# A one-core graph attention kernel: tables built during the first sort, the first load ahead of the other bins, counts read early, bf16 weight pairs and 121-wide sums

## The chip, the cores and the metric

The kernel runs on one core of a Trainium2 chip. The metric is device time in microseconds (us) of one execution.

An execution's time and its profiled span are two numbers. The span runs from the first to the last record that the profiler took; the time includes a little more. Stages are compared by spans, kernels by times.

## The reference

Four attention heads over 4,096 nodes with 64 features, and 50,000 random edges.

```python
for h in range(4):
    x_proj[h] = x @ weight[h]
src_att = sum(x_proj[h, src] * att_src[h]);  dst_att = sum(x_proj[h, dst] * att_dst[h])
score   = src_att + dst_att;  score = where(score > 0, score, 0.2 * score)
for each edge:  output[h, dst] += exp(score) * x_proj[h, src]
output[h, dst] /= (sum of exp(score) over the edges into dst) + 1e-8
```

## The kernel before

The edges become fp32 keys, 128 runs of 512, and are sorted on VectorE in two stages, with a gather of windows from memory between them, so that in the end each of 34 blocks of 121 destinations finds its edges in sixteen windows of 128, one for each group of 256 sources. Each block loads its edges, makes one-hot matrices on VectorE, gathers the source rows on TensorE with them, weighs the rows on VectorE, and sums them by destination on TensorE.

What each name in the profile is: `cnt` bounds of the windows; `raw`, `kr` the input of the second sort; `bc` a block's edges, copied to all partitions; `oh` its one-hots; `xps` gathered rows; `wv` the weights exp(score); `val` weighted rows; `Sb` the turned one-hot; `acc` the sums; `pf` the sums times the weight matrix; `res` the output rows.

```python
with tc.manual_schedule():                      # the constants above stand outside: a scheduler places them
    ...
    so.rows(1, EL)                              # first sort
    store(skey1, so.runs())
    tables(pr, pps, pp1)                        # x, weights -> xa, adb: 32 transposes, 132 small matmuls
    bounds(so1, pp1, sgn, ...)                  # cnt_ps on TensorE, cnt, ws, we on VectorE
    ...
    for i in range(NI - 1):                     # four bins of eight blocks
        win.unpack(i)                           # VectorE, then two stores on SyncE
    blocks.run(lambda: win.unpack(NI - 1))      # loads 0 to 2 first, the fifth bin after turn(0)
n1 = nc.values_load(most[0:1, 0:1], ...)        # overflow counts, read at the very end
n2 = nc.values_load(most[0:1, 1:2], ...)
with tc.If((n1 > W1) | (n2 > W2)): ...          # not taken with these edges
# --- one block, run() ---
for b in range(ND):
    self.load(b + 3); self.weigh(b); self.gather(b + 1); self.turn(b + 1); self.onehot(b + 2)
    if b: self.sink.give(b - 1)
    self.scatter(b)
# --- cuts from its parts ---
V.tensor_tensor(out=wv[:], in0=av(ex[:], 0, [1, H], [2 * H, NT], [0, 2]), ..., op=OP.max)     # fp32 ex
T.matmul(out=acc[:, k * P:(k + 1) * P], lhsT=val[:, t, k * P:(k + 1) * P], rhs=Sb[:, t, :], ...)  # 128 wide
V.tensor_scalar(out=inv[:], in0=aT[:, C:CW], scalar1=1e-8, ...); V.reciprocal(out=inv[:], in_=inv[:])
```

## Time and profile before

| | before |
|---|---|
| time, median of the first three runs | 372.82 us |
| time of the profiled run, its span | 373.68, 371.9 us |
| first sort stored | at 72.49 us |
| second sort can begin (`kr`) | at 124.91 us |
| first bin stored, first one-hot | at 169.96, 180.71 us |
| one block of the loop on VectorE | 5.26 us |

Read it in stages. Up to 72.5 us VectorE sorts, and beside it little works but ScalarE and GpSimd in the first 20 us. From there to 125 us VectorE does next to nothing. From 181 us on, a loop of 34 blocks keeps VectorE and TensorE both nearly full. A share of busy time over the whole span (VectorE 76%, TensorE 58%) shows none of this. The lines themselves stand in the prediction.

### The profile page before, as it was taken

Reading aid. Unit: us, or ns where it says so; the run is one execution under the profiler, and the core shown is the slowest. Engines: PE = TensorE matmul, PEld = TensorE weight load, DVE = VectorE, ACT = ScalarE, POOL = GpSimd, SP = SyncE. Lnnn points to the kernel's source line nnn. Section 1 sums busy time; section 2 is a strip of 40 time slices with the busy share of each in tenths; the row PEclk is TensorE's granted clock in tenths of the full one; section 3 lists DMA queues with packets and bytes.
Section 4 is the critical chain, followed back from the end, with each engine's and each line's share of the span. In section 5 each row is a group of like instructions: output and inputs, shape, how many; then the busy total and the mean of one; then the engine's idle time right before and its main releaser. Section 6 shows DMA issues by size and latency. Waiting matters only on the chain.

```text
span 371.9 us, 9662 instructions
## 1 busy us (share of the span) xinstructions
PE 215.6 (58%) x4122; PEld 206.5 (56%) x4122; DVE 282.4 (76%) x584; ACT 164.3 (44%) x290; POOL 18.9 (5%) x40
## 2 busy tenths in 40 slices
PE   0000000029996000000399999999999999999990
PEld 0000000016996000000399999999999999999980
DVE  4999999700002599974599999999999999999970
ACT  1840000015000499600086666655765566656640
POOL 2820000000000200014000000000000000000000
PEclk9999999999555555555599999999999999999996
DMA  2000000050000100002866556655675567655410
GB/s 86 1 7 0 0 0 1 28 120 0 2 0 0 29 0 0 1 28 67 345 227 223 199 220 254 239 200 208 245 250 200 205 243 254 209 203 229 143 42 20
DMA packets 13550, 43.96 MB, mean 118 GB/s; under 512 B 3308, under 2 KB 8492, under 8 KB 9148
## 3 DMA queue, kind: packets, MB, share of 16 engines
q1 hardware_dynamic: 12556, 42.22, 32.1%
q0 software_dynamic: 704, 0.66, 0.7%
q8 instruction: 34, 0.56, 0.7%
q10 hardware_dynamic: 240, 0.40, 0.3%
q14 instruction: 16, 0.13, 0.1%
HBM read 38.22 MB, written 5.05 MB: 116 GB/s over the span
## 4 chain that ended last, share of the span: by engine, by line
DVE 60%; PE 25%; DMA 6%; issue 3%; ACT 2%; SPq 1%; POOL 1%; DVEq 0%; POOLq 0%
DVE val L437 14%; DVE sA L183 11%; DVE sB L183 10%; DVE oh L390 7%; PE at_ps L335 7%; PE acc L448 7%; DVE oh L391 4%; PE sp L425 3%; DVE res L496 3%; PE xps L403 3%; DMA wS<-in_weight_dram 2%; PE xps L405 2%; PE pf L490 1%; PE ps L330 1%; DMA bc<-gat_bins 1%
## 5 line engine op out<-in xcount | busy, mean ns | idle before, releaser
L437 DVE TENSOR_TENSOR val<-xs,wv 128x4096 bf16<-128x4096 bf16 x34 | 77.9, 2292 | 4.1 <-ACT xs L412 0.6
L448 PE MATMUL acc<-Sb,val 128*128 128x128 bf16 x1088 | 79.9, 217 | 1.2
L450 PE MATMUL acc<-wv,Sb 128*128 128x4 bf16 x544 | 76.0, 168 | 0.0
L448 PEld LDWEIGHTS <-val 128*128 128x128 bf16 x1088 | 67.2, 96 | 6.3 <-DVE val L437 6.1
L426 ACT COPY Sb<-sp 128x1024 bf16<-128x1024 bf16 x68 | 66.2, 1039 | 0.0
L403 PE MATMUL xps<-xa,oh 128*128 128x72 bf16 x544 | 53.9, 194 | 15.5 <-DVE oh L390 15.5
L403 PEld LDWEIGHTS <-oh 128*128 128x128 bf16 x544 | 50.3, 98 | 15.8 <-DVE oh L390 15.8
L405 PE MATMUL xps<-xa,oh 128*128 128x72 bf16 x544 | 53.7, 195 | 0.4 <-DVE oh L391 0.4
L407 PE MATMUL xps<-adb,oh 128*128 128x8 bf16 x544 | 52.8, 169 | 0.0
L450 PEld LDWEIGHTS <-Sb 128*128 128x128 bf16 x544 | 52.1, 96 | 0.0
L407 PEld LDWEIGHTS <-oh 128*128 128x128 bf16 x544 | 50.2, 97 | 0.0
L405 PEld LDWEIGHTS <-oh 128*128 128x128 bf16 x544 | 49.6, 96 | 0.6 <-DVE oh L391 0.6
L390 DVE TENSOR_SCALAR oh<-bc,pF 128x4096 bf16<-128x4096 bf16 x34 | 43.5, 1281 | 7.0 <-DMA bc<-gat_bins 7.0
L318 PE MATMUL ps<-ident,wS 64*128 64x64 f32 x2 | 0.7, 350 | 80.8 <-DMA wS<-in_weight_dram 80.8
L318 PEld LDWEIGHTS ps<-ident,wS 64*128 64x128 f32 x2 | 0.4, 178 | 80.8 <-issue 80.8
L183 DVE TENSOR_TENSOR sA<-sB 128x256 f32<-128x256 f32 (+2 forms) x108 | 39.7, 409 | 1.8
L410 ACT ACTIVATE ex<-xps 128x128 f32<-128x128 f32 x34 | 9.4, 277 | 65.1 <-PE xps L407 65.1
L183 DVE TENSOR_TENSOR sB<-sA 128x256 f32<-128x256 f32 (+2 forms) x100 | 36.8, 409 | 1.7
L425 PE MATMUL sp<-identb,oh 128*128 128x128 bf16 x544 | 36.6, 221 | 0.0
L258 DVE TENSOR_SCALAR cnt<-cnt_ps 128x17 f32<-128x17 f32 (+1 forms) x3 | 0.5, 180 | 44.8 <-PE cnt_ps L256 44.8
L412 ACT CAST xs<-xps 128x1024 bf16<-128x1024 f32 x34 | 34.2, 1007 | 0.0
L425 PEld LDWEIGHTS <-oh 128*128 128x128 bf16 x544 | 31.5, 99 | 0.0
(115 smaller groups left out, 295.9 us busy)
## 6 DMA issues: line engine op xcount, KB each, us to landing
bc<-gat_bins SPq DMA_DIRECT2D x34, 1024.0 KB
out_dram<-res SPq DMA_DIRECT2D x33, 121.0 KB
gat_sorted<-sA SPq DMA_DIRECT2D x2, 256.0 KB
eD<-in_edge_index_dram ACTq DMA_DIRECT2D x1, 390.0 KB
eS<-in_edge_index_dram SPq DMA_DIRECT2D x1, 390.0 KB
gat_bins<-tb SPq DMA_DIRECT2D x10, 32.0 KB
out_dram<-res SPq DMA_DIRECT2D x1, 103.0 KB
win<-gat_sorted,wi POOLq DMA_INDIRECT x5, 2.5
```

Of the source, the lines that this page charges most:

```text
L183: V.tensor_tensor(out=av(d[:], o, [2 * h, n], [1, h]), in0=av(s[:], 0, [2 * h, n], [1, h]), in1=av(s[:], h, [2 * h, n], [1, h]), op=op)
L335: T.matmul(out=ps[:, b, :], lhsT=xT[:, b * step:b * step + P], rhs=uv[:, k, :], start=(b == 0), stop=True, skip_group_check=True)
L390: V.tensor_scalar(out=oh[:, 0:2, :], in0=bc[:], scalar1=pF[:, 0:1], scalar2=None, op0=OP.is_equal)
L403: T.matmul(out=o, lhsT=oh[:, 1, e], rhs=xa[:, 2 * t, :], start=(t % 4 == 0), stop=False, skip_group_check=True)
L405: T.matmul(out=o, lhsT=oh[:, 2, e], rhs=xa[:, 2 * t + 1, :], start=False, stop=False, skip_group_check=True)
L407: T.matmul(out=o[:, Din:XC], lhsT=oh[:, 0, e], rhs=adb[:, b, :], start=False, stop=True, skip_group_check=True)
L412: S.copy(out=xs[:], in_=av(xps[:], 0, [512, 4], [XC, 4], [1, Din]))
L425: T.transpose(out=sp[:, i, :], in_=oh[:, 0, t * W2:(t + 1) * W2], identity=identb[:])
L426: S.copy(out=Sb[:, q * NT // 2:(q + 1) * NT // 2, :], in_=sp[:])
L437: V.tensor_tensor(out=av(val[:], 0, [Dout, H], [C, NT], [1, Din]), in0=av(xs[:], 0, [0, H], [2, NT * Din // 2], [1, 2]), in1=av(wv[:], 0, ...
L448: T.matmul(out=acc[:, k * P:(k + 1) * P], lhsT=val[:, t, k * P:(k + 1) * P], rhs=Sb[:, t, :], start=(t == 0 and k == 0), stop=(t == NT - 1 ...
L450: T.matmul(out=acc[:, C:CW], lhsT=Sb[:, t, :], rhs=av(wv[:], 2 * t, [2 * NT, H]), start=False, stop=(t == NT - 1), skip_group_check=True)
```

## The change

Five things: the tables are built ahead of the first sort's rows in program order; the whole program, constants included, keeps its recorded order; the first bin's two stores go out on SyncE and ScalarE, then the first loads, and only then the other bins, on ScalarE; the counts are read before the blocks; and in the block `ex` and `wv` are bf16 in pairs, ScalarE adds the 1e-8, and the sums are 121 wide with the four-column ones first. (Two smaller edits go with the fifth: `xps` gets a simpler layout, and the last block's `val` is made in two halves.)

```diff
+    order = ExitStack()
+    order.enter_context(tc.manual_schedule())        # from the first instruction on
 ...
+        tables(pr, pps, pp1)
         so.rows(1, EL)
         store(skey1, so.runs())
-            tables(pr, pps, pp1)
         bounds(...)
 ...
+        n1, n2 = room(0, EL), room(1, L)
     with ExitStack() as st:
         blocks = Blocks(st, Finish(st))
-            for i in range(NI - 1):
-                win.unpack(i)
-            blocks.run(lambda: win.unpack(NI - 1))
+        win.unpack(0, nc.sync, nc.scalar)
+        for b in range(3):
+            blocks.load(b)
+        for i in range(1, NI):
+            win.unpack(i, nc.scalar, nc.scalar)
+        blocks.run()
 ...  # the block
-            V.tensor_tensor(out=wv[:], in0=av(ex[:], 0, [1, H], [2 * H, NT], [0, 2]),
-                            in1=av(ex[:], H, [1, H], [2 * H, NT], [0, 2]), op=OP.max)
+            V.tensor_tensor(out=wv[:], in0=ex[:, 0], in1=ex[:, 1], op=OP.max)
+            # val of the last block in two halves
 ...
             for t in range(NT):
+                T.matmul(out=acc[:, 2 * BD:AW], lhsT=Sb[:, t, :], rhs=av(wv[:], 2 * t, [2 * NT, H]), ...)
+            for k in range(2):
+                for t in range(NT):
+                    T.matmul(out=acc[:, k * BD:(k + 1) * BD], lhsT=val[...], rhs=Sb[:, t, 0:BD], ...)
 ...
-            V.tensor_scalar(out=inv[:], in0=aT[:, C:CW], scalar1=1e-8, scalar2=None, op0=OP.add)
-            V.reciprocal(out=inv[:], in_=inv[:])
+            S.activation(out=aT[:, 2 * BD:AW], in_=acc[:, 2 * BD:AW], func=ACTF.Identity, bias=eps[:, 0:1])
+            V.reciprocal(out=inv[:], in_=aT[:, 2 * BD:AW])
```

More of the change, by code (lines that the diff above doesn't have):

```diff
@@ L107 @@
     pm8 = bits("pm8", 0, 7)
+    eps = cst.tile([P, 1], F32)
+    V.memset(eps[:], 1e-8)
     goff = cst.tile([P, 1], F32)
@@ L275, in longest, with room @@
         V.tensor_reduce(out=most[:, k:k + 1], in_=mx_ps[:], axis=AX, op=OP.max)
+    def room(k, n):
+        return nc.values_load(most[0:1, k:k + 1], min_val=0, max_val=RUN * n,
+                              skip_runtime_bounds_check_because="a count of a run's edges")
     def fetch(pool, skey, start, n, to, what):
@@ L341 @@
     NT = NR
+    AW = 2 * BD + H
     class Windows:
@@ L351, in __init__, with unpack @@
             fetch(pool, skey2, start, W2, self.win[:].rearrange("p i e -> p (i e)"), 2)
-        def unpack(self, i):
+        def unpack(self, i, *engs):
             V.tensor_scalar(out=self.kb[:, i, :], in0=self.win[:, i, :], scalar1=boff[:, i:i + 1], scalar2=None,
@@ L360, in unpack @@
             V.tensor_copy(out=self.tb[:, i], in_=self.t[:, i])
-            for k in range(2):
-                nc.sync.dma_start(out=dataclasses.replace(bin_dram[8 * i, k],
-                                                          ap=[[2 * NR * W2, 8], [W2, NR], [1, W2]]),
-                                  in_=self.tb[:, i, k, :])
+            for k, eng in enumerate(engs):
+                eng.dma_start(out=dataclasses.replace(bin_dram[8 * i, k], ap=[[2 * NR * W2, 8], [W2, NR], [1, W2]]),
+                              in_=self.tb[:, i, k, :])
     class Blocks:
@@ L398, in gather @@
             oh = self.oh[b]
-            xps = self.psx.tile([P, 4, 512], F32, name="xps")
+            xps = self.psx.tile([P, NT, P], F32, name="xps")
             for t in range(NT):
-                o = xps[:, t // 4, (t % 4) * XC:(t % 4) * XC + XC]
+                o = xps[:, t, 0:XC]
                 e = slice(t * W2, (t + 1) * W2)
@@ L408, in gather @@
                          skip_group_check=True)
-            ex = self.bp.tile([P, NT, 2 * H], F32, name="ex")
-            S.activation(out=ex[:], in_=av(xps[:], Din, [512, 4], [XC, 4], [1, 2 * H]), func=ACTF.Exp)
+            ex = self.bp.tile([P, 2, H, NT, 2], BF16, name="ex")
+            S.activation(out=av(ex[:], 0, [2, NT], [2 * NT, 2 * H], [1, 2]),
+                         in_=av(xps[:], Din, [P, NT], [1, 2 * H], [0, 2]), func=ACTF.Exp)
             xs = self.bp.tile([P, NT, Din], BF16, name="xs")
-            S.copy(out=xs[:], in_=av(xps[:], 0, [512, 4], [XC, 4], [1, Din]))
+            S.copy(out=xs[:], in_=xps[:, :, 0:Din])
             self.ex[b], self.xs[b] = ex, xs
@@ L427, in turn, with weigh @@
             self.Sb[b] = Sb
-        def weigh(self, b):
+        def weigh(self, b, parts=1):
             xs, ex = self.xs.pop(b), self.ex.pop(b)
             wv = self.bp.tile([P, H, NT, 2], BF16, name="wv")
-            V.tensor_tensor(out=wv[:], in0=av(ex[:], 0, [1, H], [2 * H, NT], [0, 2]),
-                            in1=av(ex[:], H, [1, H], [2 * H, NT], [0, 2]), op=OP.max)
+            V.tensor_tensor(out=wv[:], in0=ex[:, 0], in1=ex[:, 1], op=OP.max)
             self.wv[b] = wv
             val = self.bp.tile([P, NT, C], BF16, name="val")
-            V.tensor_tensor(out=av(val[:], 0, [Dout, H], [C, NT], [1, Din]),
-                            in0=av(xs[:], 0, [0, H], [2, NT * Din // 2], [1, 2]),
-                            in1=av(wv[:], 0, [2, H * NT], [0, Din // 2], [1, 2]), op=OP.mult)
+            n = H // parts
+            for h in range(0, H, n):
+                V.tensor_tensor(out=av(val[:], h * Dout, [Dout, n], [C, NT], [1, Din]),
+                                in0=av(xs[:], 0, [0, n], [2, NT * Din // 2], [1, 2]),
+                                in1=av(wv[:], h * 2 * NT, [2, n * NT], [0, Din // 2], [1, 2]), op=OP.mult)
             self.val[b] = val
@@ L444, in scatter, with run @@
             val, wv, Sb = self.val.pop(b), self.wv.pop(b), self.Sb.pop(b)
-            acc = self.psa.tile([P, CW], F32, name="acc")
+            acc = self.psa.tile([P, AW], F32, name="acc")
             for t in range(NT):
-                for k in range(2):
-                    T.matmul(out=acc[:, k * P:(k + 1) * P], lhsT=val[:, t, k * P:(k + 1) * P], rhs=Sb[:, t, :],
-                             start=(t == 0 and k == 0), stop=(t == NT - 1), skip_group_check=True)
-                T.matmul(out=acc[:, C:CW], lhsT=Sb[:, t, :], rhs=av(wv[:], 2 * t, [2 * NT, H]), start=False,
+                T.matmul(out=acc[:, 2 * BD:AW], lhsT=Sb[:, t, :], rhs=av(wv[:], 2 * t, [2 * NT, H]), start=(t == 0),
                          stop=(t == NT - 1), skip_group_check=True)
+            for k in range(2):
+                for t in range(NT):
+                    T.matmul(out=acc[:, k * BD:(k + 1) * BD], lhsT=val[:, t, k * P:(k + 1) * P], rhs=Sb[:, t, 0:BD],
+                             start=False, stop=(t == NT - 1), skip_group_check=True)
             self.sink.take(b, acc[:])
-        def run(self, between=lambda: None):
-            for b in range(3):
-                self.load(b)
+        def run(self):
             self.onehot(0)
@@ L459, in run @@
             self.turn(0)
-            between()
             self.onehot(1)
@@ L463, in run @@
                 self.load(b + 3)
-                self.weigh(b)
+                self.weigh(b, 2 if b == ND - 1 else 1)
                 self.gather(b + 1)
@@ L481, in take @@
         def take(self, b, acc):
-            aT = self.fp.tile([P, CW], F32, name="aT")
-            S.copy(out=aT[:], in_=acc)
+            aT = self.fp.tile([P, AW], F32, name="aT")
+            S.copy(out=aT[:, 0:2 * BD], in_=acc[:, 0:2 * BD])
+            S.activation(out=aT[:, 2 * BD:AW], in_=acc[:, 2 * BD:AW], func=ACTF.Identity, bias=eps[:, 0:1])
             self.aT[b] = aT
@@ L489, in give @@
             for k in range(2):
-                T.matmul(out=pf[:, k * P:(k + 1) * P], lhsT=aT[:, k * P:(k + 1) * P], rhs=Wbd[:, k, :],
+                T.matmul(out=pf[0:BD, k * P:(k + 1) * P], lhsT=aT[:, k * BD:(k + 1) * BD], rhs=Wbd[:, k, :],
                          start=(k == 0), stop=True, skip_group_check=True)
             inv = self.fp.tile([P, H], F32, name="inv")
-            V.tensor_scalar(out=inv[:], in0=aT[:, C:CW], scalar1=1e-8, scalar2=None, op0=OP.add)
-            V.reciprocal(out=inv[:], in_=inv[:])
+            V.reciprocal(out=inv[:], in_=aT[:, 2 * BD:AW])
             res = self.fp.tile([P, H, Dout], F32, name="res")
-            V.tensor_tensor(out=res[:], in0=av(pf[:], 0, [Dout, H], [1, Dout]), in1=av(inv[:], 0, [1, H], [0, Dout]),
-                            op=OP.mult)
+            V.tensor_tensor(out=res[0:BD], in0=av(pf[0:BD], 0, [Dout, H], [1, Dout]),
+                            in1=av(inv[0:BD], 0, [1, H], [0, Dout]), op=OP.mult)
             n = min(BD, N - b * BD)
@@ L523, in advance @@
         return at
-    with tc.manual_schedule():
-        with tc.tile_pool(name="sort1", bufs=1) as so1, tc.tile_pool(name="pre", bufs=1) as pr, \
-                tc.tile_pool(name="pps", bufs=2, space=PSUM) as pps, \
-                tc.tile_pool(name="pp1", bufs=1, space=PSUM) as pp1:
-            sli = so1.tile([P, EL], I32)
-            tF = so1.tile([P, EL], F32)
-            uF = so1.tile([P, EL], F32)
-            key = so1.tile([P, L], F32)
-            so = Sorter(so1, key)
-            for t in (key, so.a[2]):
-                V.memset(t[:, EL:L], KPAD)
-            src = av(eS[:], 0, [2, EL])
-            dst = av(eD[:], 0, [2, EL])
-            sgn = below(so1, src, EL, nb1, NR, NR)
-            V.tensor_scalar(out=sli[:], in0=src, scalar1=SG - 1, scalar2=None, op0=OP.bitwise_and)
-            V.tensor_scalar(out=tF[:], in0=sli[:], scalar1=1.0 - N, scalar2=None, op0=OP.mult)
-            V.scalar_tensor_tensor(out=uF[:], in0=dst, scalar=float(SG), in1=tF[:], op0=OP.mult, op1=OP.add)
-            V.scalar_tensor_tensor(out=key[:, 0:EL], in0=src, scalar=float(N), in1=uF[:], op0=OP.mult, op1=OP.add)
-            so.rows(1, EL)
-            store(skey1, so.runs())
-            tables(pr, pps, pp1)
-            bounds(so1, pp1, sgn, NR, EL, [sel1[:, 0, :], sel1[:, 1, :]], off1, m16, NR, ws1, we1)
-        with tc.tile_pool(name="sort2", bufs=1) as so2, tc.tile_pool(name="pp2", bufs=1, space=PSUM) as pp2:
-            group(so2, pp2, ws1[:])
-            win = Windows(cst, ws2[:])
-            longest(so2, pp2, ws1, we1, 0)
-            longest(so2, pp2, ws2, we2, 1)
-        with ExitStack() as st:
-            blocks = Blocks(st, Finish(st))
-            for i in range(NI - 1):
-                win.unpack(i)
-            blocks.run(lambda: win.unpack(NI - 1))
@@ L559 @@
-    n1 = nc.values_load(most[0:1, 0:1], min_val=0, max_val=RUN * EL,
-                        skip_runtime_bounds_check_because="a count of a run's edges")
-    n2 = nc.values_load(most[0:1, 1:2], min_val=0, max_val=RUN * L,
-                        skip_runtime_bounds_check_because="a count of a run's edges")
+    with tc.tile_pool(name="sort1", bufs=1) as so1, tc.tile_pool(name="pre", bufs=1) as pr, \
+            tc.tile_pool(name="pps", bufs=2, space=PSUM) as pps, \
+            tc.tile_pool(name="pp1", bufs=1, space=PSUM) as pp1:
+        sli = so1.tile([P, EL], I32)
+        tF = so1.tile([P, EL], F32)
+        uF = so1.tile([P, EL], F32)
+        key = so1.tile([P, L], F32)
+        so = Sorter(so1, key)
+        for t in (key, so.a[2]):
+            V.memset(t[:, EL:L], KPAD)
+        src = av(eS[:], 0, [2, EL])
+        dst = av(eD[:], 0, [2, EL])
+        sgn = below(so1, src, EL, nb1, NR, NR)
+        V.tensor_scalar(out=sli[:], in0=src, scalar1=SG - 1, scalar2=None, op0=OP.bitwise_and)
+        V.tensor_scalar(out=tF[:], in0=sli[:], scalar1=1.0 - N, scalar2=None, op0=OP.mult)
+        V.scalar_tensor_tensor(out=uF[:], in0=dst, scalar=float(SG), in1=tF[:], op0=OP.mult, op1=OP.add)
+        V.scalar_tensor_tensor(out=key[:, 0:EL], in0=src, scalar=float(N), in1=uF[:], op0=OP.mult, op1=OP.add)
+        tables(pr, pps, pp1)
+        so.rows(1, EL)
+        store(skey1, so.runs())
+        bounds(so1, pp1, sgn, NR, EL, [sel1[:, 0, :], sel1[:, 1, :]], off1, m16, NR, ws1, we1)
@@ new lines @@
+    with tc.tile_pool(name="sort2", bufs=1) as so2, tc.tile_pool(name="pp2", bufs=1, space=PSUM) as pp2:
+        group(so2, pp2, ws1[:])
+        win = Windows(cst, ws2[:])
+        longest(so2, pp2, ws1, we1, 0)
+        longest(so2, pp2, ws2, we2, 1)
+        n1, n2 = room(0, EL), room(1, L)
+    with ExitStack() as st:
+        blocks = Blocks(st, Finish(st))
+        win.unpack(0, nc.sync, nc.scalar)
[4 more added lines that the diff above has]
+        blocks.run()
@@ L563 @@
+    order.close()
     with tc.If((n1 > W1) | (n2 > W2)):
         with tc.tile_pool(name="all", bufs=1) as al:
-            total = al.tile([P, ND, CW], F32)
+            total = al.tile([P, ND, AW], F32)
             V.memset(total[:], 0.0)
@@ L571 @@
                     longest(so3, pp3, ws2, we2, 1)
-                m2 = nc.values_load(most[0:1, 1:2], min_val=0, max_val=RUN * L,
-                                    skip_runtime_bounds_check_because="a count of a run's edges")
+                m2 = room(1, L)
                 with tc.For_i(0, m2, W2):
@@ L577 @@
                         for i in range(NI):
-                            win.unpack(i)
-                        Blocks(st, Total(total)).run()
+                            win.unpack(i, nc.sync, nc.scalar)
+                        blocks = Blocks(st, Total(total))
+                        for b in range(3):
+                            blocks.load(b)
+                        blocks.run()
             with ExitStack() as st:
```

## The prediction

> **What bounds the kernel now.** I read the page's slices first, then the chain of work that ended last, then the timeline around each place where the chain leaves VectorE, then one block of the main loop on each engine. The span is 371.9 us, the timed median 372.82, so 0.95 us is added at the end of the sum.
>
> ```profile
> PE   0000000029996000000399999999999999999990
> DVE  4999999700002599974599999999999999999970
> ACT  1840000015000499600086666655765566656640
> PEclk9999999999555555555599999999999999999996
> ```
>
> Each digit is 9.3 us. VectorE is full except in slices 8 to 12, where TensorE and ScalarE work alone, and around slice 18. So the program is: first sort (VectorE), a stage without VectorE, second sort (VectorE), a handover, 34 blocks. The chain names the stage without VectorE:
>
> ```profile
> 73.06 0.88 SPq L302
> 73.98 6.69 DMA wS<-in_weight_dram
> 85.33 3.43 PE ps L330 x16
> 90.06 26.61 PE at_ps L335 x132
> ```
>
> The tables (load of x and the weights, transposes, 132 small matmuls) begin when the first sort is stored and hold the chain until 116.7. VectorE waits for one matmul that stands behind them in TensorE's queue:
>
> ```profile
> 117.25 0.18 DVE L258 TENSOR_SCALAR cnt<-cnt_ps 128x17 f32<-128x17 f32 x1 [44.78 <-PE cnt_ps L256]
> 119.71 0.17 DVE L281 CAST wi<-ws 128x2 int32<-128x2 f32 x1
> 120.70 1.06 POOL L283 DMA_INDIRECT raw<-gat_sorted,wi  x1 [100.12 <-DVE wi L281]
> 124.91 0.49 DVE L291 TENSOR_SCALAR kr<-raw,goff 128x512 f32<-128x512 f32 x1 [5.03 <-DMA raw<-gat_sorted,wi]
> ```
>
> The handover after the second sort: eight stores of bins go out one after another on SyncE, and only then the first block's load.
>
> ```profile
> 169.96 5.25 SPq L362 DMA_DIRECT2D gat_bins<-tb  x8
> 175.65 1.28 SPq L382 DMA_DIRECT2D bc<-gat_bins  x3
> 180.71 1.29 DVE L390 TENSOR_SCALAR oh<-bc,pF 128x4096 bf16<-128x4096 bf16 x1 [6.97 <-DMA bc<-gat_bins]
> ```
>
> The main loop, one block on VectorE (val to val is 269.85 - 264.59 = 5.26 us, with no wait bracket anywhere):
>
> ```profile
> 266.80 1.28 DVE L390 TENSOR_SCALAR oh<-bc,pF 128x4096 bf16<-128x4096 bf16 x1
> 267.99 0.75 DVE L391 TENSOR_SCALAR oh<-bc,pF 128x2048 bf16<-128x2048 bf16 x1
> 268.65 0.16 DVE L493 TENSOR_SCALAR inv<-aT 128x4 f32<-128x4 f32 x1
> 268.85 0.18 DVE L494 RECIPROCAL inv<-inv 128x4 f32<-128x4 f32 x1
> 269.12 0.42 DVE L496 TENSOR_TENSOR res<-pf,inv 128x256 f32<-128x256 f32 x1
> 269.46 0.28 DVE L433 TENSOR_TENSOR wv<-ex 128x128 bf16<-128x128 f32 x1
> 269.85 2.29 DVE L437 TENSOR_TENSOR val<-xs,wv 128x4096 bf16<-128x4096 bf16 x1
> ```
>
> TensorE is busy 99.33 of the 100 us from 200 to 300, which reads like the bound, but the wait list shows it waiting for val in 26 blocks:
>
> ```profile
> PEld L448 <- DVE val L437: 6.1, 26, 0.3
> ```
>
> Its own pace is in block 1, where it did not wait: gather at 191.52, transposes 192.97, pf 193.86, acc 194.36, next gather 196.56, that is 1.44 + 0.89 + 0.50 + 2.21 = 5.04 us. Later the pf part reads 0.71 instead of 0.50; the difference of 0.21 is the wait for val. The chain switches to TensorE at 314, but there pf still lasts 0.71, so I take VectorE as the bound of the whole loop, with TensorE 0.22 us behind it.
>
> **What the Trainium skill says.** "VectorE: DVE Perf Modes", the perf-mode tier table: tensor_tensor runs at twice the rate only when all operands are bf16. The trace agrees: val takes 2292 ns for 4096 bf16 elements (0.56 ns each) and 256 fp32 elements of the sort about 0.42 us. "TensorE: Matmul & The Clock Gate", back-to-back issue gap: N columns cost N/2.4 + 2.5 ns warm, with a floor of about 25 ns start to start. Here 128-column matmuls start 55 ns apart and the 8-column ones of the gather hold 25 ns. "DMA: Bandwidth & Descriptors", issuing engines are not separate DMA queues: a second issuing engine saves only issue time. Here that is what is scarce: 0.6 us per bin store. Same page, why a DMA increments its semaphore by 16: the number of DMA engines must divide the outermost size, so a prime count of rows goes through one engine. The last output has 4096 - 33 x 121 = 103 rows; the trace's DMA records show its 103 packets of 1 KB in single file from 364.58 to 369.61.
>
> **The change part by part.**
>
> (1) Tables into the first sort. All their work is on SyncE, POOL, TensorE and ScalarE; VectorE does none. ScalarE's 16 counts (0.77 us each) end near 19 us; the tables then need what they needed before, 117.2 - 80.8 = 36.4 us, perhaps 42 if TensorE's clock is at half for the transposes too: done at 56 to 62, before the sort's end at 72.5. What stays after the sort is the bounds and the fetch: 117.25 to wi's end 119.88 is 2.63, wi's end to the fetch's issue 0.82, issue to kr 4.21, total 7.66 us. The store of the keys (issued 72.49, last packet 74.17) lies inside the first two. Before, sort's end to kr was 124.91 - 72.49 = 52.42. Saved: 52.42 - 7.66 = 44.8 us.
>
> (2) Recorded order from the top. Before, a scheduler put some 35 small constants into VectorE's stream in the middle of the sort, 9.15 to 11.40: 2.25 us on the path. Now they stand ahead of it, and VectorE is idle until the edges land (5.25). In program order more of them depend on the one before (about 0.19 us start to start against 0.07), so they need about 4.5 us from 1.0 on and may run 0.3 to 0.5 past the landing. The load of x may delay eD a little. Saved: 1.8 us.
>
> (3) First load ahead of the other bins. The first store still goes at 169.96; its packets landed about 171.55; SyncE has some eight old waits to step through (0.065 us each, most passed by then), so the load goes near 171.85 instead of 175.65: 3.8 us. Against it: the other bins' eight stores (ScalarE's queue) and the last window fetch share the DMA engines with this load, some 0.6 us. Unpacking the fifth bin earlier is free: VectorE is done by 175.1. Saved: 3.2 us. What follows the first one-hot is tied to TensorE at half clock, and keeps its length.
>
> (4) Overflow counts early. At the end they are not on the path: SyncE's register reads end at 365.9, its branch waits for instructions until 368.9, and the last output lands after 369.6. Early, they fall where VectorE and SyncE wait for the window (166.9 to 168.9). Saved: nothing, lost: nothing.
>
> (5) The loop. VectorE loses the add of 1e-8 (268.65 to 268.85: 0.197 us) and wv drops from fp32 to dense bf16: 128 elements at about 1.09 ns, from the sort's 0.42 and 0.36 us for 256 and 196, halve, 0.07 us. 5.26 - 0.27 = 5.0 us. TensorE: 32 matmuls of 121 columns instead of 128 save 32 x 2.9 ns = 0.09 us, so about 4.95, and the 16 four-column sums now stand first and need no val, so they hide in the wait. ScalarE gets a wider exp (256 instead of 128 outputs, about 0.1 us) and a second small op on the sums (about 0.2), on top of 0.38 + 0.28 + 1.01 + 1.95 = 3.6 of 5.26: still free. Two engines within 0.05 us of each other will rub a little: I take 5.02. There are 32 such periods: 32 x 0.24 = 7.7 us.
>
> (6) The end. The last val in halves lets the first half of its matmuls start 1.15 us sooner, but TensorE also does block 32's sums and pf in between. Stepping through it: wv of block 33 to res is 6.31 us now (357.08 to 363.39); after it, half a val's matmuls are hidden, ScalarE's extra op costs some of it: saved 0.4. From res on, the 103-row output and the teardown (8.0 us) stay.
>
> Sum: 44.8 + 1.8 + 3.2 + 0 + 7.7 + 0.4 = 57.9. 372.8 - 57.9 = 314.9 us.
>
> **The rivals.** (A) TensorE becomes the bound of the loop: if the sixteen four-column matmuls with a weight load each, now back to back, took 50 ns instead of 27, its block would be 5.3 us, the loop would gain nothing and the time would be 322. Against it: in the gather three weight loads pass in 90 ns. (B) TensorE and VectorE are so close that they trade waits at 5.1: 317. (C) The tables don't fit under the sort, for instance because ScalarE starts them late: each us beyond 72.5 comes back; 10 us of room speaks against it. (D) The first load waits for more than its bin, or crawls behind the bin stores: up to 2.5 us back, 317. (E) The reading in (4) is wrong and early counts free the end: up to 2 us less, 313. (F) VectorE alone sets 4.97 with no rub and the constants fit wholly under the landing: 312.5.
>
> **Range and chances.** The 45 us of (1) are safe unless C holds. What is open is the loop (0.1 us per block is 3.2 us), the handover (1 to 1.5) and the start (1), so 311.5 to 319.0. A result within 2% of before would need (1) to fail wholly.
>
> **What would show it.** In the changed profile: VectorE's idle before cnt gone and some 5 us before kr left; the small table matmuls between about 25 and 62; first sort beginning near 5.7; the first load issued near 171.85 less 46.6, that is 125, and oh near 131; val to val 5.0 with TensorE waiting for val at most 0.1 per block; the last output again 8 us before the end. Val to val at 5.2 would make (5) wrong and A or B right; an idle VectorE before cnt, C; a load issued late, D.

## The result, and the profile after

The changed kernel takes 317.05 us (median of 4, 316.97 to 317.14); the kernel before, beside it, 372.98 us (median of 4). The ratio is 0.8496, 95% interval 0.8480 to 0.8512. A ratio is the mean time of one kernel's fast runs over that of the other's of the same rounds, so it isn't quite the ratio of the medians. The predicted 314.9 us was 2.1 us too low, and within its range of 311.5 to 319.0.

Both spans, cut at the same eight events, in us:

| stage | before | after | saved | predicted |
|---|---|---|---|---|
| start to first sort stored | 72.49 | 70.47 | 2.02 | 1.8 |
| to `kr` | 52.42 | 7.56 | 44.86 | 44.8 |
| to first bin's store | 45.05 | 45.00 | 0.05 | 0 |
| to first one-hot | 10.75 | 8.82 | 1.93 | 3.2 |
| to `wv` of block 1 | 9.82 | 10.23 | -0.41 | 0 |
| to `wv` of block 33 | 166.56 | 158.22 | 8.34 | 7.7 |
| to last `res` | 6.31 | 5.96 | 0.35 | 0.4 |
| to the end of the span | 8.51 | 8.65 | -0.14 | 0 |
| sum | 371.9 | 314.9 | 57.0 | 57.9 |

The slices of the changed kernel, a fortieth of its span each:

```profile
PE   0049999000000000099999999999999999999970
DVE  8999999993999995479999999999999999999960
ACT  3984000000999600067777768677686767768640
PEclk9999555555555555579999999999999999999995
```

TensorE's tables now lie in slices 2 to 6, under a full VectorE. The hole of VectorE has shrunk to slice 9. On TensorE's timeline these are the table matmuls and the four matmuls behind them that VectorE had waited 44.78 us for (start, duration, engine, line, operation, shapes):

```profile
28.51 25.22 PE L345 MATMUL at_ps<-uv,xT 64*128 64x4 f32 x132
53.66 1.03 PE L261 MATMUL cnt_ps<-sgn,sel 128*128 128x17 f32 x4
```

They end at 54.7, 16 us before the sort does. On VectorE's timeline after the sort, brackets are waits:

```profile
70.36 0.17 DVE L263 TENSOR_SCALAR cnt<-cnt_ps 128x17 f32<-128x17 f32 x1
72.82 0.17 DVE L291 CAST wi<-ws 128x2 int32<-128x2 f32 x1
78.03 0.49 DVE L301 TENSOR_SCALAR kr<-raw,goff 128x512 f32<-128x512 f32 x1 [5.04 <-DMA raw<-gat_sorted,wi]
```

`cnt` has lost its bracket; only the fetch's 5.04 us stays. (`cnt` begins slightly before the store is issued at 70.47.)

The handover, from SyncE's, ScalarE's and VectorE's timelines ("SPq" and "ACTq" are DMA issues):

```profile
123.03 0.72 SPq L373 DMA_DIRECT2D gat_bins<-tb  x1
125.87 10.79 SPq L392 DMA_DIRECT2D bc<-gat_bins  x5
```
```profile
123.03 6.57 ACTq L373 DMA_DIRECT2D gat_bins<-tb  x9
```
```profile
131.85 1.29 DVE L400 TENSOR_SCALAR oh<-bc,pF 128x4096 bf16<-128x4096 bf16 x1 [3.68 <-DMA bc<-gat_bins]
```

The load follows the first store after 2.84 us instead of 5.69, but it takes 5.98 us to the one-hot instead of 5.06.

One block of the loop on VectorE:

```profile
217.25 2.29 DVE L449 TENSOR_TENSOR val<-xs,wv 128x4096 bf16<-128x4096 bf16 x1
219.46 1.28 DVE L400 TENSOR_SCALAR oh<-bc,pF 128x4096 bf16<-128x4096 bf16 x1
220.65 0.75 DVE L401 TENSOR_SCALAR oh<-bc,pF 128x2048 bf16<-128x2048 bf16 x1
221.31 0.17 DVE L504 RECIPROCAL inv<-aT 128x4 f32<-128x4 f32 x1
221.58 0.42 DVE L506 TENSOR_TENSOR res<-pf,inv 121x256 f32<-121x256 f32 x1
221.92 0.21 DVE L444 TENSOR_TENSOR wv<-ex 128x128 bf16<-128x128 bf16 x1
222.24 2.29 DVE L449 TENSOR_TENSOR val<-xs,wv 128x4096 bf16<-128x4096 bf16 x1
```

`val` to `val` is 222.24 - 217.25 = 4.99 us, still with no bracket: the add is gone and `wv` is 0.07 us shorter. But TensorE has no waits in the loop either. Its timeline early in the loop (the 32 wide sums of a block) shows a pitch of 4.95 us, shorter than VectorE's:

```profile
150.70 1.87 PE L463 MATMUL acc<-Sb,val 128*128 128x121 bf16 x32
155.65 1.87 PE L463 MATMUL acc<-Sb,val 128*128 128x121 bf16 x32
160.60 1.87 PE L463 MATMUL acc<-Sb,val 128*128 128x121 bf16 x32
```

and the chain that ended last (start, length, what), which begins at 228 us and lies on TensorE throughout, a pitch of 4.98:

```profile
230.25 1.73 PE acc L463 x32
...
235.23 1.72 PE acc L463 x32
```

An engine can't have a shorter pitch than the one it waits for. So early in the loop TensorE is behind and catches up at its own 4.946 us, and later VectorE's 4.987 sets the pitch. Which of the two costs time if it gets slower the profile alone does not tell: both look like the bound. That was the first thing to test.

### The profile page after: what moved, and what is told of

Read it like the earlier page. It is cut to its first block, busy times and chain, and to the rows that moved or that the text cites. A ratio compares the mean times of both kernels' runs of the same rounds, so it can differ in the third digit from the quotient of the medians.

```text
span 314.9 us, 9697 instructions
## 1 busy us (share of the span) xinstructions
PE 207.2 (66%) x4122; PEld 202.2 (64%) x4122; DVE 275.9 (88%) x552; ACT 172.9 (55%) x324; POOL 18.6 (6%) x40
## 5 line engine op out<-in xcount | busy, mean ns | idle before, releaser
L449 DVE TENSOR_TENSOR val<-xs,wv 128x4096 bf16<-128x4096 bf16 (+1 forms) x35 | 78.0, 2231 | 4.1 <-ACT xs L423 0.7
L463 PE MATMUL acc<-Sb,val 128*128 128x121 bf16 x1088 | 63.6, 217 | 0.0
L463 PEld LDWEIGHTS <-val 128*128 128x128 bf16 x1088 | 58.5, 98 | 0.1
L420 ACT ACTIVATE ex<-xps 128x256 bf16<-128x256 f32 x34 | 13.4, 395 | 58.3 <-PE xps L417 58.3
L250 ACT ACTIVATE junk<-kr,nb 128x512 f32<-128x512 f32 x34 | 24.5, 722 | 25.6 <-DVE kr L301 24.5
L261 PE MATMUL cnt_ps<-sgn,sel 128*128 128x17 f32 (+1 forms) x6 | 1.7, 390 | 53.1 <-ACT sgn L253 53.1
L261 PEld LDWEIGHTS cnt_ps<-sgn,sel 128*128 128x128 f32 x6 | 1.4, 318 | 53.2 <-issue 53.2
L401 DVE TENSOR_SCALAR oh<-bc,pF 128x2048 bf16<-128x2048 bf16 x34 | 25.4, 747 | 0.0
L345 PEld LDWEIGHTS at_ps<-uv,xT 64*128 64x128 f32 x132 | 25.1, 297 | 0.4 <-issue 0.4
```

Of the source, the lines that this page charges most:

```text
L345: T.matmul(out=ps[:, b, :], lhsT=xT[:, b * step:b * step + P], rhs=uv[:, k, :], start=(b == 0), stop=True, skip_group_check=True)
L401: V.tensor_scalar(out=oh[:, 2, :], in0=bc[:, 1, :], scalar1=pF[:, 1:2], scalar2=None, op0=OP.is_equal)
L449: V.tensor_tensor(out=av(val[:], h * Dout, [Dout, n], [C, NT], [1, Din]), in0=av(xs[:], 0, [0, n], [2, NT * Din // 2], [1, 2]), in1=av(wv[ ...
L463: T.matmul(out=acc[:, k * BD:(k + 1) * BD], lhsT=val[:, t, k * P:(k + 1) * P], rhs=Sb[:, t, 0:BD], start=False, stop=(t == NT - 1), skip_g ...
```

## The experiments

Eleven runs. "Changed" is the changed kernel. The runs were on three occasions with the kernel before beside them each time (medians 373.28, 373.64 and 373.63 us), so across occasions the ratios are compared: 0.8496 for the changed kernel, and 0.001 is 0.37 us. The intervals of the ratios are 0.0012 to 0.0023 wide to each side.

### One part alone: the tables

```diff
# the kernel before
+            tables(pr, pps, pp1)
             so.rows(1, EL)
             store(skey1, so.runs())
-            tables(pr, pps, pp1)
```

> The kernel before with one part of the change alone: the tables are built ahead of the first sort's rows. My theory (the tables fit wholly under the sort and their 44.8 us come off one for one): 372.9 - 44.8 = 328.1 us, sort's end to kr 7.6 us. Rival (the tables' ScalarE and DMA work disturbs the sort, or the scheduler that is still on in this version places them late): 330 to 340 us. Rival (the parts of the change are not additive, the other parts gained more because of this one): below 327.

329.34 us (3 rounds), ratio 0.8822, which is 44 us less than before. VectorE's timeline after its sort, stored at 72.64:

```profile
72.53 0.17 DVE L258 TENSOR_SCALAR cnt<-cnt_ps 128x17 f32<-128x17 f32 x1
74.99 0.17 DVE L281 CAST wi<-ws 128x2 int32<-128x2 f32 x1
80.22 0.49 DVE L291 TENSOR_SCALAR kr<-raw,goff 128x512 f32<-128x512 f32 x1 [5.06 <-DMA raw<-gat_sorted,wi]
```

Store to `kr` is 7.58 us, as in the changed kernel: this part does its 44.8 us alone (the time says 43.9, the upper end of its interval 44.7). The sort itself still ends at 72.6; the 2 us that the changed kernel gains there are not the tables', and are left for the order of the constants: in this trace they still stand in the middle of the sort, from 9.31 to 11.56 us.

### Which engine bounds the loop

Slow VectorE, or slow TensorE, and see which counts.

```diff
# changed: the add back on VectorE (a second 1e-8, for its time)
-            V.reciprocal(out=inv[:], in_=aT[:, 2 * BD:AW])
+            V.tensor_scalar(out=inv[:], in0=aT[:, 2 * BD:AW], scalar1=1e-8, scalar2=None, op0=OP.add)
+            V.reciprocal(out=inv[:], in_=inv[:])
```

> The changed kernel with an extra add of 1e-8 on VectorE in each block, 0.197 us as in the kernel before. Theory (VectorE bounds the loop): 33 x 0.197 = 6.5 us more, 323.5 us, val to val 5.18 us. Rival (TensorE's 4.946 us is what paces the loop and VectorE has room): under 3 us more, below 320 us.

323.03 us (3 rounds), ratio 0.8641: 5.4 to 6.0 us more. In the trace `wv` 1 to `wv` 33 took 164.67 instead of 158.22 us, 6.45 more, with 5.19 us per block. VectorE's slack is nil.

```diff
# changed: ex and wv in fp32 as before the change
-            ex = self.bp.tile([P, 2, H, NT, 2], BF16, name="ex")
+            ex = self.bp.tile([P, NT, 2 * H], F32, name="ex")
 ...
-            V.tensor_tensor(out=wv[:], in0=ex[:, 0], in1=ex[:, 1], op=OP.max)
+            V.tensor_tensor(out=wv[:], in0=av(ex[:], 0, [1, H], [2 * H, NT], [0, 2]), ..., op=OP.max)
```

> The changed kernel with the weights in fp32 as in the kernel before (ex and wv fp32, wv 128 elements with a strided output), all else kept. Theory (VectorE bounds the loop and wv's 0.07 us counts in full): 34 x 0.066 = 2.2 us more, 319.2 us. Rival (TensorE paces the loop, wv's saving was hidden): 317.1 to 317.5 us. Rival (the wider exp had cost ScalarE something on the path): at most 317.

318.82 us (5 rounds), ratio 0.8528: 1.2 to 1.8 us more. The block's period was 5.055 us, 0.066 longer as expected; the loop 1.73 us longer, because this profile had no late load and the changed kernel's had one of 0.43.

```diff
# changed: sums 128 wide again, nothing else
-    AW = 2 * BD + H
+    AW = 2 * P + H
-  T.matmul(out=acc[:, k * BD:(k + 1) * BD], lhsT=val[:, t, k * P:(k + 1) * P], rhs=Sb[:, t, 0:BD], ...)
+  T.matmul(out=acc[:, k * P:(k + 1) * P],   lhsT=val[:, t, k * P:(k + 1) * P], rhs=Sb[:, t, :], ...)
```

> The changed kernel with sums 128 columns wide instead of 121 (32 matmuls per block, 7 columns each more). From the trace of the changed kernel TensorE's own block is 4.946 us and VectorE's val to val 4.987 us. Theory (the two engines stand so close that TensorE becomes the bound): 4.946 + 32 x 2.9 ns = 5.04 us, 0.05 us more per block, 318.7 us. Rival (VectorE has the last word, TensorE's extra 0.09 us lies in its wait for val): 317.1 to 317.4 us. Rival (the two rub, each TensorE ns counts in full): 0.09 x 33 = 3 us, 320 us.

319.31 us (5 rounds), ratio 0.8549: 2.0 to 2.3 us more. TensorE's block was 5.027 us, VectorE's 4.987 for some twenty blocks and 5.027 after that. The wait list of VectorE in the loop and its end, changed kernel and this one (engine, line, releaser: us in total, times, longest):

```profile
DVE res L506 <- PE pf L501: 0.4, 1, 0.4
```
```profile
DVE res L506 <- PE pf L501: 2.6, 3, 2.0
```

and VectorE's timeline near the end of the wide version:

```profile
300.93 0.17 DVE L504 RECIPROCAL inv<-aT 128x4 f32<-128x4 f32 x1
303.08 0.42 DVE L506 TENSOR_TENSOR res<-pf,inv 121x256 f32<-121x256 f32 x1 [1.99 <-PE pf L501]
```

TensorE falls 0.04 us further behind in each block, the double buffers hide it for twenty blocks, and then VectorE waits; at the end, where VectorE has no more one-hots to make and would run ahead, it stands 1.99 us for `pf`. So both engines bound this loop within 0.041 us of each other: by the traces a us more on VectorE costs nearly its whole, and of the 2.6 us that the wide sums add on TensorE (32 x 0.081) 2.0 to 2.3 came through. The narrower sums were not needed for the loop to gain, but without them that much of its 8.34 us would have been lost.

### The first load

```diff
# changed: all ten bin stores on SyncE, ahead of the loads
-        win.unpack(0, nc.sync, nc.scalar)
+        for i in range(NI):
+            win.unpack(i, nc.sync, nc.sync)
         for b in range(3):
             blocks.load(b)
-        for i in range(1, NI):
-            win.unpack(i, nc.scalar, nc.scalar)
```

> The changed kernel with all ten bin stores issued on SyncE ahead of the first block's load, as before the change. Theory (the load ahead of the bins is worth what it moved, less what the shared DMA engines cost): eight issues of some 0.6 us come back ahead of the load and the load's own flight shrinks by up to 0.9 us: about 2.9 us more, 320 us. Rival (only the 1.93 us by which the handover shrank between the two profiles come back): 319 us. Rival (the load's place does not matter): 317.1 us.

320.26 us (3 rounds), ratio 0.8567: 2.65 us more by the ratio. First store to first one-hot was 11.75 us, 2.93 more than changed. This is a little harder than the kernel before, which had eight stores ahead of the load and not ten, so it is not the exact undoing. SyncE's timeline:

```profile
123.44 6.52 SPq L373 DMA_DIRECT2D gat_bins<-tb  x10
130.39 1.28 SPq L392 DMA_DIRECT2D bc<-gat_bins  x3
```

The load's own flight, 130.39 to the one-hot at 135.18, was 4.79 us, against 5.98 in the changed kernel. One pair of profiles overstates this: in the seven traces with the other bins on ScalarE the flight was 5.20 to 6.05 us, in the four without 4.79 to 5.12, so company costs the load about 0.8 us. In the same seven traces the load was issued 2.54 to 3.47 us after the first store, and the one-hot came 8.34 to 8.96 us after it: half a us between two profiles says nothing here.

```diff
# changed: bins 1 to 4 stored by SyncE, so behind the first three loads
         for i in range(1, NI):
-            win.unpack(i, nc.scalar, nc.scalar)
+            win.unpack(i, nc.sync, nc.sync)
```

> The changed kernel with bins 1 to 4 stored by SyncE behind the first three loads, instead of by ScalarE beside them. Theory (the load lost 0.95 us because ScalarE's store took long to issue beside SyncE's, and 0.9 us because bin stores and window fetch share the DMA engines with it): 0.5 to 0.9 us less, 316.2 us. Rival (the load's flight is set by its own reading from memory, not by the company): 317.1 us. Rival (the second and third load get later and hold the one-hot of block 1): above 317.5 us.

317.14 us (5 rounds, 316.55 to 317.81), ratio 0.8488, interval 0.8472 to 0.8504: by time this can't be told from the changed kernel. In the trace the theory holds in part: the load's flight fell from 5.98 to 4.90 us, but the load was still issued 2.61 us after the first store (2.84 in the changed kernel), and of the 1.31 us by which the first one-hot came nearer to the first store, only 0.80 reached block 1's `wv`. Where did 0.5 us go? TensorE's weight loads of the first block ("PEld", brackets are waits), changed kernel first, then this one:

```profile
133.19 0.10 PEld L413 LDWEIGHTS <-oh 128*128 128x128 bf16 x1 [13.88 <-DVE oh L400]
134.15 0.11 PEld L415 LDWEIGHTS <-oh 128*128 128x128 bf16 x1 [0.85 <-DVE oh L401]
```
```profile
132.03 0.10 PEld L413 LDWEIGHTS <-oh 128*128 128x128 bf16 x1 [12.57 <-DVE oh L400]
133.49 0.11 PEld L415 LDWEIGHTS <-oh 128*128 128x128 bf16 x1 [1.36 <-DVE oh L401]
```

The first weight load waits for the first part of the one-hot and goes at once (1.34 us after the one-hot began). The second comes 0.96 and 1.46 us later, and the bracket blames the second part of the one-hot; but that one had ended: it ran from 131.89 for 0.75 us in this trace. What stands between are TensorE's two register reads of the counts, at 133.18 and 133.78 in the changed kernel (0.50 and 0.31 us), at 132.02 and 132.72 here (0.60 and 0.71 us). The bracket names the wrong releaser. The built program has TensorE's queue in this order, though the source has the reads first:

```
L279 Matmult mx_ps<-ident,mxr
L413 Ldweights oh
L284 TensorLoad most x2
L413 Matmult xps<-xa,oh
```

The build has put the weight load of the block's first matmul ahead of the reads. It waits for the one-hot, the reads wait behind it, and the matmul waits behind the reads.

### The counts

```diff
# changed: the counts read after the blocks, as before the change
-        n1, n2 = room(0, EL), room(1, L)
 ...
         blocks.run()
     order.close()
+    n1, n2 = room(0, EL), room(1, L)
```

> The changed kernel with the two overflow counts read into the registers after the 34 blocks again, as before the change. My theory: the early read costs the first gather 0.3 to 0.4 us, because TensorE reads two registers between its first weight load and its first matmul, and at the end the late read is hidden by the 103-row output in single file: 316.7 us, 0.35 less than the changed kernel. Rival (early counts are worth what the change meant them to be, some 2 us of reads at the end): 319 us. Rival (no difference either way): 317.05.

316.75 us (5 rounds, 316.71 to 317.61), ratio 0.8484, interval 0.8468 to 0.8501. The time alone does not decide it. In the trace the first one-hot to `wv` 1 took 9.93 instead of 10.23 us; block 0's first two matmuls came 1.34 and 2.00 us after the one-hot began, instead of 2.26 and 2.30. At the end SyncE's reads pushed its branch from 0.99 to 2.43 us after the last `res` began, and the branch's instructions from 3.84 to 4.97; the last output's landing was noticed at 6.82 and 6.87. So the early reads cost 0.3 us and gain nothing, as long as the output is last. (First one-hot to `wv` 1 was 10.12 to 10.73 us in all seven traces with TensorE's reads in that place, and 9.93 in all four without. The profiled run, 317.61, also had four longer blocks: two waited 0.51 and 0.54 us for a load, which comes and goes between runs, and two 0.36 us at `res`. These two stand in the same blocks in split_last_late, the other trace with late counts, and in no other; why is open.)

To see what the early counts are worth, the output has to be taken out of the way. The last block has 103 rows.

```diff
# changed: the last output in two transfers
-            nc.sync.dma_start(out=out[b * BD:b * BD + n, :], in_=res[0:n].rearrange("p h o -> p (h o)"))
+            for r0, r1 in (((0, n),) if n == BD else ((0, 96), (96, n))):
+                nc.sync.dma_start(out=out[b * BD + r0:b * BD + r1, :], in_=res[r0:r1].rearrange("p h o -> p (h o)"))
```

> The changed kernel with the last output (103 rows) as two transfers, 96 rows and 7 rows. Theory (the 103 packets in single file of 5.3 us set the end; 96 rows spread over 16 DMA engines and 7 packets take under 1 us, after which SyncE's branch, ready 3 us after the last result, sets the end): about 2.6 us less, 314.4 us. Rival (the branch and its teardown set the end already): 317.1 us. Rival (the second issue of about 0.6 us on SyncE delays the branch in its turn): 315 us.

314.83 us (5 rounds), ratio 0.8429: 2.2 to 2.5 us less. The 103 packets of 1 KB had taken from 307.45 to 312.73; in 96 and 7 rows they took from 307.52 to 309.01. Issuing the second transfer delayed SyncE's branch by 0.45 us, and from then on the branch was last: its instructions came at 310.50, the last check of a semaphore was passed at 311.84.

> The changed kernel with the last output in 96 and 7 rows, and the overflow counts read after the blocks again. Theory (with the output out of the way the branch sets the end, and now the early counts are worth what the late reads take on SyncE): in the run with late counts alone SyncE had its branch's instructions 4.97 us after the last result began, plus 0.37 us for the second output's issue = 5.34; with the split alone it was 4.26 us: 1.1 us later; the early read's 0.3 us in the prologue comes off: 314.5 + 1.1 - 0.3 = 315.3 us. Rival (the reads are hidden whatever the output does): 314.2 us. Rival (the reads cost the full 2 us): 316.4 us.

315.75 us (5 rounds), ratio 0.8445: 0.6 to 0.9 us more than with the split alone, where the theory had 0.8. By time that isn't clear of the noise (0.0016 between ratios whose intervals are 0.0019 and 0.0012 wide to each side); the trace carries it. The branch's instructions came 5.00 us after `res` instead of 4.26, and 0.3 us came back in the prologue. So with the output split the early counts save 0.74 us at the end for 0.3 in the prologue; in the changed kernel as it is they save nothing.

### The reads away from the first matmul, and all together

```diff
# changed + bins 1 to 4 behind the loads, and a transpose that nobody reads
         n1, n2 = room(0, EL), room(1, L)
+        idle_ps = pp2.tile([1, P], F32, name="idle_ps")
+        T.transpose(out=idle_ps[:], in_=eps[:], identity=ident[:])
```

> The changed kernel with bins 1 to 4 stored behind the first three loads, and with one small transpose that nobody reads on TensorE after the count reads, so that this transpose's weight load, and not block 0's, is what TensorE does ahead of the reads. Theory (in the run with the bins behind, TensorE's two register reads of 0.60 and 0.71 us began only when block 0's weights were loaded, and the first matmul came 2.77 us after the first one-hot began, against 2.26 in the changed kernel): the reads move into the wait for the load, the first matmul comes 1.4 to 2.0 us after the one-hot, and the time is 0.6 us less than with the bins behind alone: 316.1 us. Rival (the reads still stand behind block 0's weights, or something else holds the first matmul): 316.7 us, as with the bins behind. Rival (the loop is TensorE's and it is the half clock that holds block 1): 316.7 us with an early first matmul.

316.01 us (5 rounds, 6 runs), ratio 0.8457: 1.1 us less than with the bins behind alone. TensorE's weight loads:

```profile
120.66 0.08 PEld L563 LDWEIGHTS idle_ps<-ident,eps 128*1 128x1 f32 x1 [0.99 <-issue]
132.12 0.10 PEld L413 LDWEIGHTS <-oh 128*128 128x128 bf16 x1 [11.38 <-DVE oh L400]
132.78 0.10 PEld L415 LDWEIGHTS <-oh 128*128 128x128 bf16 x1 [0.56 <-DVE oh L401]
```

The unread transpose's matmul now stands between the reads and block 0's weight load, and the build left that load behind it. The reads happen at 119.58 and 120.32, inside the wait for the window. The second weight load comes 0.66 us after the first, which is the second part of the one-hot and nothing else. One-hot to `wv` 1 is 9.93 us, as with late counts.

```diff
# the same, with the split output and four load buffers
-            self.bcp = pool(name="bc", bufs=3)
+            self.bcp = pool(name="bc", bufs=4)
+            self.load(3)
             for b in range(ND):
-                self.load(b + 3)
+                self.load(b + 4)
```

> The version that the runs point to: last output in 96 and 7 rows, bins 1 to 4 behind the loads, reads ahead of block 0's weights, and four instead of three buffers for the loads, each issued one block earlier (VectorE waited for a late load 0.3 to 1.4 us in all in the profiles). Theory (the gains add): 314.5 - 0.3 to 0.8 - 0.6 - 0.4 = 312.7 to 313.2 us. Rival (the longer lead of the loads makes the first ones slower, or the gains in the prologue are lost because TensorE still enters the loop late): 313.8 to 314.5 us.

313.43 us (5 rounds, 312.77 to 314.02), ratio 0.8377: by the ratios 1.4% or 4.4 us less than the changed kernel. It beats both kernels. The gains add within the scatter, though not each is seen in this profile, which is that of the slowest of the five runs: the one-hot came 8.28 us after the first store here, against 7.39 and 7.51 in the two other traces with the bins behind. What the fourth buffer does is not shown: no block was late in this profile, but none was in the profile before it either, with three.

## Why the prediction was right

The size held: faster by 15%, of which the tables' part is four fifths. By its own steps:

(1) Tables: 44.8 predicted, 44.86 in the trace, and the run with this part alone agrees. The room was larger than the 10 us reckoned with: ScalarE began them at 19 us, right after its counts, as assumed, and they ended at 54.

(2) The recorded order: 1.8 predicted, 2.02 measured. The sort step that began at 11.40 us, behind the constants, now begins at 9.57, so 1.83 us of it lie there. No run moved the constants alone.

(3) The first load: 3.2 predicted, 1.93 measured. This is the term that was mis-sized. The mechanism is right (with the bins ahead again, 2.9 us come back), and two sizes in it were wrong. "Its packets landed about 171.55", "so the load goes near 171.85" gave 1.89 us from store to load; it was 2.84 (2.54 at the least in the other traces). A block reads both halves of its bin, so the second half's landing counts, at 125.04, 2.0 us after the first store was issued; ScalarE needed 1.16 us to issue it where SyncE needed 0.72 beside it. And a landing isn't a release: SyncE passed that wait at 125.56, 0.53 us after the last packet, and four more checks of semaphores took it to 125.87. The Trainium skill says this of a DMA issued by GpSimd, on "DMA: Bandwidth & Descriptors", in the anatomy of one DMA: the semaphore can't fire until the last byte is confirmed in the target memory. The 0.53 us after a store from ScalarE fits that; the prediction left it out. The second size: the flight of the load beside the other bins, 0.6 us dearer in the prediction, was 0.9 dearer than before in this profile (0.1 to 1.0 in the seven traces).

Inside the same step stood that "what follows the first one-hot ... keeps its length". It got 0.41 us longer, 0.3 of it because of (4).

(4) The early counts: nothing gained is right, and late_counts with split_last and split_last_late show why: the 103-row output, which the prediction saw in the DMA records, hides them. Nothing lost is wrong by 0.3 us. The reads were placed by the prediction where VectorE and SyncE wait; TensorE was left out, on which the built order has them behind a weight load that waits for the one-hot. That order could have been read before the run.

(5) The loop: 5.02 us a block predicted, 4.987 measured, no rub. The two engines do lie 0.041 us apart, as worked out (0.05), and rival B's trading of waits did not come: the buffers carry one engine's lag for twenty blocks. Rival D happened in small, in step 3. Rival A fell: the sixteen four-column matmuls with a weight load each take 0.419 us, 26 ns each.

(6) The end: 0.4 predicted, 0.35 measured. No run took the halves of the last `val` back alone.

The last 1.2 us are in how the sum was turned into a time. "0.95 us is added" set a span of one run against the median of others. The profiled run itself had timed 373.68, so 1.8 us belong on the span, and 2.2 in the changed kernel. Predicted span 371.9 - 57.9 = 314.0, measured 314.9: 0.9 off, and 1.2 from this. That the span is only 0.9 off is in part luck: step 3 and what follows it were 1.7 us too hopeful, the loop and the start 0.9 us too cautious.

## What to carry to other kernels

When work of idle engines stands on the chain only because of its place in program order, move it under the long stage first; one such move outweighed everything else here, and it came out to 0.1 us because every stage after it kept its length. Before trusting "no waits" on two engines, slow each of them by a known amount: in this loop both had none, and both counted. When a small job is moved early, follow it on every engine that takes part, and when a wait at the end goes away unnoticed, ask what hid it: here one output of 103 rows set the end, cost 2.2 to 2.5 us itself, and hid what the early counts save.

## What the Trainium skill lacked or had wrong

- "TensorE: Matmul & The Clock Gate", back-to-back issue gap: it gives about 81 ns per pair of weight load and matmul at N = 128 as the sustained rate in a real kernel. Here such pairs sustain 55.7 ns (32 pairs of 128 columns in 1.783 us) and 53.2 ns with 121 columns (1.703 us), which is what its formula for an isolated matmul gives. Its floor of about 25 ns holds with a full weight load to each matmul: 26 ns for the four-column ones.
- The same page, the clock gate: it ties the full clock to a busy engine. In the tables TensorE, by the profile, was busy without a gap with fp32 matmuls of four columns, and the granted clock, whose records begin at 28.73 us at full, still fell to half 3.41 us later and stayed there; their starts went from 112 to 213 ns apart. From the changed kernel's stages (us, busy time and instructions by engine, clock, DMA share, GB/s):

```profile
24.00:32.00 8.00, 8.00 (x53) 6.19 (x51) 7.62 (x22) 3.47 (x6) 0.00 (x0) 1.00 0.00 0
33.00:53.00 20.00, 20.00 (x96) 20.00 (x95) 19.14 (x48) 0.45 (x2) 0.00 (x0) 0.50 0.00 0
```

- "DMA: Bandwidth & Descriptors", latency and other measured facts: it gives a floor of about 600 ns for a register's load from memory. The reads of the counts, one value each, took 0.31 and 0.50 us on TensorE in ten of the thirteen traces (0.51 to 0.71 in the other three), and 0.28 to 0.89 us on SyncE.
- "Advanced Engine Details and Errata", control flow timing: a compare-and-branch is given as about 108 ns. SyncE's branch itself took 0.05 us here, but its next instruction came 2.5 to 3.0 us after it began, in all thirteen traces, and with the output out of the way this sets the end. No page has a time for that. "Runtime: NRT & Kernel Launch", instruction fetch mechanics, does tell of a stall while a taken branch's target is fetched; whether it is that stall was not tested.
- "DMA: Bandwidth & Descriptors", issuing engines are not separate DMA queues: it says that a second issuing engine saves only issue time. Here the saving was smaller than that too: ScalarE's first store took 1.16 to 1.34 us to issue while SyncE issued one in 0.72, and 0.6 us each after that. Whether the company or its being ScalarE's first store for 120 us is the cause was not separated.
